# Up projections and first Strassen products of a two-branch attention step: other block order, weight tiles of two blocks, first sums on VectorE

## The chip, the cores and the metric

The kernel runs on one core of one Trainium2 chip. The metric is device time in microseconds (us) of one execution. A core has TensorE (PE; PEld is its weight loads), VectorE (DVE), ScalarE (ACT), GpSimd (POOL) and SyncE (SP), whose queue issues nearly all DMAs. Each engine works through its own list of instructions in order, and waits on semaphores for the others.

## The reference, cut to what matters

One layer of a decoder with two linear-attention branches over 1024 prompt tokens and 64 sample tokens (1088 columns in the kernel, which keeps features on the 128 partitions and tokens along the free dimension). The part that the change touches:

```
y_a = (o_a * silu(z_a)) @ w_up_gla          # 512 -> 1024
y_b = (o_b * silu(z_b)) @ w_up_gdn          # 512 -> 1024
merged = sigmoid(gate_a) * y_a + sigmoid(gate_b) * y_b
h = h + merged @ w_out                      # 1024 -> 1024
h = h + sigmoid(h @ w_ple_gate) * (p @ w_ple)
```

What goes before it (projections, the two recurrences) and after it (the last two lines, and a final RMS norm) is in the program too, and is left as it is.

## The kernel before, in words

**Products in three parts.** All matmuls are made in a reduced-precision fp32 form. A matrix is split into a high part (rounded by ScalarE, `A.copy`) and a low part (the difference, by VectorE), and a product takes three matmuls per block of 128 rows: high by high, high by low, low by high. So every operand of TensorE costs one ScalarE and one VectorE instruction beforehand. The helper for activations is `parts` (lines 1335 to 1337: L1336 the high part on ACT, L1337 the low part on DVE); that for weights is `w_split` (L174 and L175), which also starts the load of a later raw weight tile (`w_load`, L167). There are two raw weight tiles (`wr`) and three of each split kind (`wh`, `wl`).

**Up projections** (`up_block`, 16 calls). The 1024 output features are eight blocks m of 128, the branch is br (0 is GLA, 1 is gated DeltaNet), the columns are three chunks: c = 0 and 1 of 416, c = 2 of 256. One call handles one (br, m): it takes one split weight tile of 4 blocks (128x512), and for each chunk loads the gate that was spilled to DRAM earlier (`gt`, a buffer called strip, of which there are eight), makes 12 matmuls into a PSUM bank (`py`), and lets DVE apply the gate: for br = 0 one instruction writes the merged tile M (or Me for chunk 2; L1403); for br = 1 one multiplies (L1405) and one adds onto M (L1406). The list `UPS` sets the order of calls. Before, it is: blocks 0 and 4 of branch 0, then of branch 1; blocks 1 and 5 likewise; then blocks 2, 6, 3, 7 of branch 0, then the same four of branch 1.

**Strassen operands** (`m_parts`, L1408). The output projection `merged @ w_out` of the first 832 columns is done as a Strassen-Winograd product: 2x2 quadrants of M and of the weights, seven products instead of eight. The quadrants of M for row block j are b11, b12 (m = j, chunks 0 and 1) and b21, b22 (m = j + 4). `m_parts(j)` makes four sums T1 to T4 of them on GpSimd (`T`, L1414 to L1421) and splits seven operands (names `M11`, `MT2`, `MT3`, `MT1`, `M21`, `MT4`, `M22` with j behind), and splits the two blocks of chunk 2 (`M2h`, `M2l`). It can run only when blocks j and j + 4 of both branches are done, for j = 3 after the last up projection.

**Strassen products** (the loop over j that follows, line 1463 on). For each of four output row pairs j, TensorE makes the seven products in the order 1, 6, 7, 5, 2, 4, 3 (`s`, L1456, 12 matmuls each over the row blocks k = 0 to 3) with plain products for chunk 2 between them (`se`, `sf`, L1461). The weight quadrants are summed in `s_weights(j)`, on GpSimd (`sw`, L1358 to L1363), in four steps that `s_next` asks for. DVE and GpSimd combine the products with the residual x (strips again, loaded at L1469; adds on GpSimd at L1483, the rest on DVE at L1480).

**Order.** From the end of the first block of projections on, a scheduler at build time orders each engine's list by the order of the source and by dependencies. Buffers with the same tag are handed on when their last reader is done, and the next writer waits for that reader.

Of the kernel before, what the change touches and what calls it, by code (L numbers as in the profile page):

```python
# [17 lines left out]
P = 128  # L18
# [3 lines left out]
CH = [(0, 384), (384, 384), (768, 320)]  # L22
ORDER2 = (5, 6, 7, 0, 1, 2, 3, 4)
LCH = [(0, 416), (416, 416), (832, 256)]
UPS = [(i // 2 % 2, i // 4 + 4 * (i % 2)) for i in range(8)] + [(i // 4, 2 + i // 2 % 2 + 4 * (i % 2)) for i in range(8)]
EPS = 1e-6
NBLK = 34
NWARM = 3
# [76 lines left out]
def tile_hybrid_step(ctx: ExitStack, tc: tile.TileContext, xT, x0, pT, wqk, wmain, wv0, wv1, wup, wout, wpg, wpl, wgate,  # L105
# [16 lines left out]
    def unit(name, dt=F32):  # L122
        return up.tile([P, UW], dt, tag="u", name=name)
# [1186 lines left out]
    lp = ctx.enter_context(tc.tile_pool(name="lp", bufs=1))  # L1310

    assert len(gscr) == 16
    wlist += [(wup[8 * br + m], 4, P, hw_main) for br, m in UPS]
    wlist += [(wout[m], 8, P, None) for j in range(4) for m in (j, j + 4)]
    w_load()
    w_load()
# [18 lines left out]
    def parts(h, l, src):  # L1335
        A.copy(h, src)  # L1336
        V.tensor_tensor(l, src, h.bitcast(F32), op=ALU.subtract)  # L1337
# [5 lines left out]
    def s_weights(j):  # L1343

        r1, r2 = wraw.pop(0)[0], wraw.pop(0)[0]
        a11, a12, a21, a22 = r1[:, 0:4], r1[:, 4:8], r2[:, 0:4], r2[:, 4:8]
        s1, s2 = (lp.tile([P, 512], F32, tag="sw", name=f"sw{j}{i}", bufs=3).rearrange("p (k n) -> p k n", n=P) for i in range(2))

        def two(x, y):
            hl = hw_main(8, P)  # L1350
            out = []
            for i, z in enumerate((x, y)):
                h, l = (t[:, 4 * i:4 * i + 4] for t in hl)
                parts(h, l, z)
                out.append((h, l))
            return out

        G.tensor_tensor(s1, a21, a22, op=ALU.add)  # L1358
        G.tensor_tensor(s2, s1, a11, op=ALU.subtract)
        yield two(a11, s2)  # L1360
        G.tensor_tensor(a11, a11, a21, op=ALU.subtract)
        yield two(a11, s1)
        G.tensor_tensor(s2, a12, s2, op=ALU.subtract)  # L1363
        yield two(a12, a22)
        q = two(s2, a21)
        if j < 3:
# [17 lines left out]
    M2 = [lp.tile([P, 8, 256], F32R, tag="xb", name=f"M2{n}", bufs=2) for n in "hl"]  # L1384

    def mcols(m, c):
        o, w = LCH[c]
        return M[m][:, o:o + w] if c < 2 else Me[m // 4][:, w * (m % 4):w * (m % 4) + w]

    def up_block(br, m, og, prefetch):  # L1390
        us = w_next()
        if br == 0:
            M[m] = unit(f"M{m}") if m % 4 > 1 else lp.tile([P, 2 * W1], F32, tag="bs", name=f"M{m}", bufs=16)
        for c, (o, w) in enumerate(LCH):
            t = strip(f"gt{br}{m}{c}", w)
            load(t, gscr[f"{'gh'[br]}{m}"][:, o:o + w])
            if c == 0:
                prefetch()
            py = pps(f"py{br}{m}{c}")
            prod(py, w, us, 0, lambda k: og[0][k][:, o:o + w], lambda k: og[1][k][:, o:o + w], 4)  # L1400
            d = mcols(m, c)
            if br == 0:
                V.scalar_tensor_tensor(d, t, 1.0, py[:, :w], op0=ALU.add, op1=ALU.mult)  # L1403
            else:
                V.scalar_tensor_tensor(t, t, 1.0, py[:, :w], op0=ALU.add, op1=ALU.mult)  # L1405
                V.tensor_tensor(d, d, t, op=ALU.add)  # L1406

    def m_parts(j):  # L1408

        b11, b12, b21, b22 = mcols(j, 0), mcols(j, 1), mcols(j + 4, 0), mcols(j + 4, 1)  # L1410
        r = {p: Mp[p].__setitem__(j, pair(f"M{p}{j}", j > 1)) or Mp[p][j] for p in Mp}
        parts(*r["11"], b11)
        t1, t2, t3, t4 = (wide(f"T{i}{j}")[:, :W1] for i in range(4))
        G.tensor_tensor(t1, b12, b11, op=ALU.subtract)  # L1414
        G.tensor_tensor(t2, b22, t1, op=ALU.subtract)
        parts(*r["T2"], t2)
        G.tensor_tensor(t3, b22, b12, op=ALU.subtract)
        parts(*r["T3"], t3)
        parts(*r["T1"], t1)
        parts(*r["21"], b21)  # L1420
        G.tensor_tensor(t4, b21, t2, op=ALU.subtract)  # L1421
        parts(*r["T4"], t4)
        parts(*r["22"], b22)
        for m in (j, j + 4):
            parts(M2[0][:, m], M2[1][:, m], mcols(m, 2))

    og = [split_pairs(oa, "oga"), split_pairs(ob, "ogb")]
    for br in range(2):
        for c in range(3):
            og[br][2](c)  # L1430
    for i, (br, m) in enumerate(UPS):
        if i == 0:
            w_split()
        up_block(br, m, og[br], w_split if i < 15 else s_next)
        if br == 1 and m > 3:
            m_parts(m - 4)
    s_next()
    s_next()


    H, He = [None] * 8, [None] * 2
# [5 lines left out]
        return H[m][:, o:o + w] if c < 2 else He[m // 4][:, w * (m % 4):w * (m % 4) + w]  # L1447

    def h_parts(m, c):
        Hp[c][m] = pair(f"H{m}{c}", c == 1 and m < 2)  # L1450
        parts(*Hp[c][m], hcols(m, c))

    def s_prod(ps, a, b):
# [9 lines left out]
    for j in range(4):  # L1463
        last = j == 3
        x11, x12, x21, x22 = (strip(f"x{m}{c}") for m in (j, j + 4) for c in (0, 1))
        xe = [strip(f"x{m}2", 256) for m in (j, j + 4)]
        for t, m, c in ((x11, j, 0), (xe[0], j, 2), (x22, j + 4, 1), (x21, j + 4, 0), (xe[1], j + 4, 2), (x12, j, 1)):
            o, w = LCH[c]
            load(t, xT[m][:, o:o + w])  # L1469
        for m in (j, j + 4):  # L1470
            H[m] = lp.tile([P, 2 * W1], F32, tag="bs", name=f"H{m}", bufs=16) if j == 0 else unit(f"H{m}")
            if j == 0:
                He[m // 4] = lp.tile([P, UW], F32, tag="M", name=f"He{m // 4}", bufs=2)
        p1, u2, u3 = (wide(f"{n}{j}")[:, :W1] for n in ("p1", "u2", "u3"))

        def ps_(n):
            return pps(f"s{n}{j}")[:, :256 if n in "ef" else W1]

        def half_of(out, ps, x):
            V.scalar_tensor_tensor(out, ps, 0.5, x, op0=ALU.mult, op1=ALU.add)  # L1480

        def add(t, x):
            G.tensor_tensor(t, t, x, op=ALU.add)  # L1483

        (a11, s2) = queue.pop(0)
        ps = ps_("1")
        s_prod(ps, a11, "11")
        A.mul(p1, ps, 0.5)
        add(x11, p1)
        e = ps_("e")  # L1490
        c_prod(e, a11, 0, True)
        ps = ps_("6")
        s_prod(ps, s2, "T2")
        half_of(u2, ps, p1)
        s_next()
        (s3, s1) = queue.pop(0)
        ps = ps_("7")
        s_prod(ps, s3, "T3")
        half_of(u3, ps, u2)
        for t, u in ((x22, u3), (x12, u2), (x21, u3)):  # L1500
            add(t, u)
        ps = ps_("5")
        s_prod(ps, s1, "T1")
        half_of(hcols(j + 4, 1), ps, x22)
        half_of(x12, ps, x12)
        if last:
            pr = [unit(f"pr{k}") for k in range(2)]
            for k in range(2):
                load(pr[k][:, :T], pT[k])
            wlist += [(wpg[0], 8, P, hw_main)]  # L1510
# [12 lines left out]
        half_of(hcols(j, 0), ps, x11)
        if last:
            h_parts(3, 0)
        c_prod(e, a12, 4, False)
        half_of(hcols(j, 2), e, xe[0])
        ps = ps_("4")
        s_prod(ps, a22, "T4")
        half_of(hcols(j + 4, 0), ps, x21)  # L1530
        e = ps_("f")
        c_prod(e, a22, 4, True)
        if last:
            h_parts(7, 0)
# [12 lines left out]
        if not last:
            s_next()
# [124 lines left out]
def _layout(i):  # L1673
# [16 lines left out]
    def vcols(m):  # L1690
# [55 lines left out]
```

## Time and profile before

| what | value |
|---|---|
| three timed runs | median 1003.38 us (1003.37 to 1005.02) |
| the profiled execution | 1005.65 us, of which the span from the first to the last instruction is 1003.8 |
| granted TensorE clock, mean | 0.995 |
| busy: PE | 986.2 us, 98% of the span |
| busy: PEld | 953.7 us, 95% |
| busy: DVE | 655.4 us, 65% |
| busy: ACT | 414.4 us, 41% |
| busy: POOL | 94.4 us, 9% |
| DMA | 84.74 MB, mean 84 GB/s |

PE is busy nearly throughout, so the shares of the other engines say little by themselves: what matters is where PE stands still, or runs slowly, and who let it wait. A row of a timeline reads: start in us, duration, engine, line, operation, output <- inputs, and in brackets the idle time before it with the engine that ended it. A row of groups reads: count | busy us, mean ns of one | idle before. A row of stretches reads: from:to in us, length, then busy us (and instructions) of PE, PEld, DVE, ACT and POOL, the granted TensorE clock, the share of DMA, GB/s.

### The profile page before, as it was taken

The page shows a single profiled execution, that of the slowest core. Times are in us where ns is not written, and L with a number is a line of the kernel's source. Part 1 is how long each engine was busy: PE and PEld are TensorE (multiplying, and loading weights), DVE is VectorE, ACT ScalarE, POOL GpSimd, SP SyncE. Part 2 cuts the span into 40 slices and gives each one's busy share as a digit, 9 for nine tenths or more (in the row PEclk, how much of TensorE's full clock was granted, in tenths as well). Part 3 has the DMA queues.
Part 4 walks back from the last instruction along what each step waited for, and adds up shares of the span by engine and source line. Part 5 has one row for each costly group of instructions (what it writes and reads, how often), then busy time and mean ns, then how long its engine had stood idle before and what let it go on. Part 6 is the DMA issues. An engine that isn't in the chain of part 4 may idle for free.

```text
span 1003.8 us, 17776 instructions
## 1 busy us (share of the span) xinstructions
PE 986.2 (98%) x6968; PEld 953.7 (95%) x6968; DVE 655.4 (65%) x1441; ACT 414.4 (41%) x997; POOL 94.4 (9%) x107
## 2 busy tenths in 40 slices
PE   9999999999999999999999999999999799999996
PEld 8999999999999989899999999999999799999996
DVE  6885745332748959867876775567767855854356
ACT  7764634432524424452264323243223222643354
POOL 0000011010000000010001000000213553100000
PEclk9999999999999999999999999999999899999999
DMA  9011112231222130322132222014453333421024
GB/s 322 5 43 64 51 53 72 84 97 70 80 78 65 35 97 22 116 74 60 60 97 73 63 86 81 12 45 144 139 151 107 102 95 95 150 84 43 22 89 153
DMA packets 66395, 84.74 MB, mean 84 GB/s; under 512 B 27316, under 2 KB 51320, under 8 KB 66312
## 3 DMA queue, kind: packets, MB, share of 16 engines
q1 hardware_dynamic: 66024, 83.22, 26.7%
q8 instruction: 55, 0.90, 0.4%
q10 hardware_dynamic: 288, 0.39, 0.1%
q14 instruction: 28, 0.23, 0.1%
HBM read 65.38 MB, written 18.21 MB: 83 GB/s over the span
## 4 chain that ended last, share of the span: by engine, by line
PE 93%; DVE 4%; issue 1%; POOL 1%; ACT 0%; DVEq 0%; POOLq 0%
PE ing L290 12%; PE ingsh L290 10%; PE eg L290 10%; PE ingsg L290 9%; PE py L290 7%; PE s L1456 6%; PE inzb L290 5%; PE inza L290 5%; PE ep L290 2%; PE inka L290 2%; PE inqa L290 2%; PE v L406 2%; PE v L407 2%; PE v L409 2%; PE sf L1461 1%
## 5 line engine op out<-in xcount | busy, mean ns | idle before, releaser
L174 ACT CAST wh<-wr 128x1024 fp32r<-128x1024 f32 (+1 forms) x67 | 63.2, 947 | 130.5 <-PE py L290 42.8
L175 DVE TENSOR_TENSOR wl<-wr,wh 128x1024 fp32r<-128x1024 f32 (+1 forms) x67 | 74.9, 1119 | 63.8 <-ACT wh L174 63.0
L290 PE MATMUL ing<-xh,wh 128*128 128x384 f32 (+1 forms) x288 | 97.1, 337 | 0.0
L290 PE MATMUL ing<-xh,wl 128*128 128x384 f32 (+1 forms) x288 | 94.8, 329 | 0.0
L290 PE MATMUL ing<-xl,wh 128*128 128x384 f32 (+1 forms) x288 | 94.6, 329 | 0.0
L290 PE MATMUL eg<-H,wh 128*128 128x416 f32 x256 | 69.3, 351 | 0.0
L290 PE MATMUL ingsg<-xh,wh 128*128 128x384 f32 (+1 forms) x192 | 66.4, 346 | 0.0
L290 PE MATMUL ingsh<-xh,wh 128*128 128x384 f32 (+1 forms) x192 | 66.2, 345 | 0.0
L290 PE MATMUL ingsg<-xl,wh 128*128 128x384 f32 (+1 forms) x192 | 63.2, 329 | 0.0
L290 PE MATMUL ingsh<-xl,wh 128*128 128x384 f32 (+1 forms) x192 | 62.9, 328 | 0.0
L290 PE MATMUL ingsg<-xh,wl 128*128 128x384 f32 (+1 forms) x192 | 62.9, 327 | 0.0
L290 PE MATMUL ingsh<-xh,wl 128*128 128x384 f32 (+1 forms) x192 | 62.8, 327 | 0.0
L290 PEld LDWEIGHTS ing<-xh,wh 128*128 128x128 f32 x288 | 54.2, 188 | 0.9 <-issue 0.7
L290 PEld LDWEIGHTS ing<-xl,wh 128*128 128x128 f32 x288 | 54.2, 188 | 0.5 <-issue 0.5
L290 PEld LDWEIGHTS ing<-xh,wl 128*128 128x128 f32 x288 | 54.1, 188 | 0.2 <-issue 0.2
L798 DVE SCALAR_TENSOR_TENSOR D<-R,cw,D 128x1112 f32<-128x1112 f32 x36 | 49.3, 1369 | 2.4 <-ACT D L796 2.1
L290 PEld LDWEIGHTS eg<-H,wh 128*128 128x128 f32 x256 | 47.7, 188 | 0.3
L290 PE MATMUL eg<-H,wl 128*128 128x416 f32 x128 | 44.6, 348 | 0.0
L953 DVE TENSOR_TENSOR tm<-B 34x30 f32<-34x30 f32 (+14 forms) x120 | 38.3, 319 | 7.4 <-DMA B<-scra 5.3
L1456 PE MATMUL s<-MT,wh 128*128 128x416 f32 x128 | 36.8, 369 | 3.2 <-DVE MT L1337 2.1
L955 DVE TENSOR_TENSOR B<-B,tm 34x30 f32<-34x30 f32 (+14 forms) x120 | 38.2, 318 | 1.8
L290 PEld LDWEIGHTS ingsg<-xh,wh 128*128 128x128 f32 x192 | 36.2, 188 | 2.2 <-issue 1.7
(491 smaller groups left out, 2899.3 us busy)
## 6 DMA issues: line engine op xcount, KB each, us to landing
wr<-in_wmain SPq DMA_DIRECT2D x38, 512.0 KB, 3.5
wr<-in_wpg SPq DMA_DIRECT2D x13, 512.0 KB, 3.6
wr<-in_wup SPq DMA_DIRECT2D x16, 256.0 KB, 2.9
wr<-in_wout SPq DMA_DIRECT2D x8, 512.0 KB, 3.8
gt<-gscrg SPq DMA_DIRECT2D x16, 208.0 KB, 2.5
gt<-gscrh SPq DMA_DIRECT2D x16, 208.0 KB, 3.0
x<-in_xT SPq DMA_DIRECT2D x16, 208.0 KB, 2.4
out_yT<-y SPq DMA_DIRECT2D x8, 416.0 KB, 4.1
```

Of the source, the lines that this page charges most:

```text
L174: a = A.copy(wh, wr).ins
L175: b = (eng or V).tensor_tensor(wl, wr, wh.bitcast(F32), op=ALU.subtract).ins
L290: mm(ps[:, :w], l_, r_, start=i == 0, stop=i == len(seq) - 1)
L406: mm(ps[:, :n], h_, a_, start=k == 0, stop=False)
L407: mm(ps[:, :n], l_, a_, start=False, stop=False)
L409: mm(ps[:, :n], h_, b_, start=False, stop=k == 7)
L798: V.scalar_tensor_tensor(D[:, :n], R[:, i:n + i], cw[:, 4 * ci + i:4 * ci + i + 1], D[:, :n], op0=ALU.mult, op1=ALU.add)
L953: V.tensor_tensor(tv, Bv[:, j:j + 1, j + 1:32].broadcast_to([NBLK, j, n]), Bv[:, 0:j, j:j + 1].broadcast_to([NBLK, j, n]), op=ALU.mult)
L955: V.tensor_tensor(Bv[:, 0:j, j + 1:32], Bv[:, 0:j, j + 1:32], tv, op=ALU.add)
L1456: mm(ps, a[p_][:, k], Mp[b][k][q_], start=(k, i) == (0, 0), stop=(k, i) == (3, 2))
L1461: mm(ps, a[p_][:, k], M2[q_][:, k0 + k], start=first and (k, i) == (0, 0), stop=not first and (k, i) == (3, 2))
```

## The change

Five things are changed.

1. `UPS` now has eight entries (br, j) in the order (0,0), (1,0), (0,1), (1,1) and so on, and `up_pair` handles blocks j and j + 4 in one call, with one weight tile of 8 blocks (128x1024; the array is laid out anew on the host). Within a call the chunks come as (j,0), (j,1), (j+4,0), (j+4,1), (j,2), (j+4,2).
2. `m_parts` runs after each branch 1 call; its T sums go to VectorE; for j = 2 it splits 21 and 22 first, otherwise in the order in which the products need them, with the weight steps put between for j = 3.
3. The weight sums of `s_weights(0)` and the residual adds of j = 0 go to VectorE; j = 1 to 3 stay on GpSimd.
4. For j = 3 the merged tiles M take four of the eight strips. Other buffers move between pools.
5. Two weight steps that stood behind the up projections are asked for inside the last `m_parts`.

```
-UPS = [(i // 2 % 2, i // 4 + 4 * (i % 2)) for i in range(8)] + [(i // 4, 2 + i // 2 % 2 + 4 * (i % 2)) for i in range(8)]
+UPS = [(0, 0), (1, 0), (0, 1), (1, 1), (0, 2), (1, 2), (0, 3), (1, 3)]
-    wlist += [(wup[8 * br + m], 4, P, hw_main) for br, m in UPS]
+    wlist += [(wup[4 * br + j], 8, P, hw_main) for br, j in UPS]
...
+        E_ = V if j == 0 else G
-        G.tensor_tensor(s1, a21, a22, op=ALU.add)
-        G.tensor_tensor(s2, s1, a11, op=ALU.subtract)
+        E_.tensor_tensor(s1, a21, a22, op=ALU.add)
+        E_.tensor_tensor(s2, s1, a11, op=ALU.subtract)
...
-    def up_block(br, m, og, prefetch):
+    def up_pair(br, j, og, prefetch):
         us = w_next()
-        if br == 0:
-            M[m] = unit(f"M{m}") if m % 4 > 1 else lp.tile([P, 2 * W1], F32, tag="bs", name=f"M{m}", bufs=16)
-        for c, (o, w) in enumerate(LCH):
+        for m in (j, j + 4) if br == 0 else ():
+            if j == 3:
+                M[m] = [strip(f"M{m}{c}") for c in range(2)]
+            else:
+                t = unit(f"M{m}") if j == 2 else lp.tile([P, 2 * W1], F32, tag="bs", name=f"M{m}", bufs=16)
+                M[m] = [t[:, c * W1:c * W1 + W1] for c in range(2)]
+        for i, (m, c) in enumerate(((j, 0), (j, 1), (j + 4, 0), (j + 4, 1), (j, 2), (j + 4, 2))):
...
-            prod(py, w, us, 0, lambda k: og[0][k][:, o:o + w], lambda k: og[1][k][:, o:o + w], 4)
+            prod(py, w, us, m // 4 * 4, lambda k: og[0][k][:, o:o + w], lambda k: og[1][k][:, o:o + w], 4)
...
+        def put(p, src):
+            Mp[p][j] = pair(f"M{p}{j}", j == 3 or j == 2 and p not in ("21", "22"))
+            parts(*Mp[p][j], src)
+
+        if j == 2:
+            put("21", b21)
+            put("22", b22)
+        put("11", b11)
+        V.tensor_tensor(t1, b12, b11, op=ALU.subtract)
+        V.tensor_tensor(t2, b22, t1, op=ALU.subtract)
+        put("T2", t2)
         for m in (j, j + 4):
             parts(M2[0][:, m], M2[1][:, m], mcols(m, 2))
+        yield
+        V.tensor_tensor(t3, b22, b12, op=ALU.subtract)
+        put("T3", t3)
+        put("T1", t1)
+        yield
...
-    for i, (br, m) in enumerate(UPS):
-        if i == 0:
-            w_split()
-        up_block(br, m, og[br], w_split if i < 15 else s_next)
-        if br == 1 and m > 3:
-            m_parts(m - 4)
-    s_next()
-    s_next()
+    w_split()
+    for i, (br, j) in enumerate(UPS):
+        up_pair(br, j, og[br], w_split if i < 7 else s_next)
+        if br == 1:
+            for _ in m_parts(j):
+                if j == 3 and len(queue) < 3:
+                    s_next()
...
-            G.tensor_tensor(t, t, x, op=ALU.add)
+            (V if j == 0 else G).tensor_tensor(t, t, x, op=ALU.add)
```

TensorE's list holds the same number of instructions as before, and the Strassen products stand in the same order. The lists of the other engines move. Two places on VectorE are shown as the built programs have them, before and after apart.

The first is VectorE's list around the last up projections. In the names, `py172` is the product of branch 1, block 7, chunk 2, the last one; `gt172` is its gate; `M113` is the low part of operand 11 for j = 3, `MT23` that of T2; `Me1` and `M2l` belong to chunk 2; `wl` are low parts of weights. Before:

```order
L1405 SCALAR_TENSOR_TENSOR gt170_8446<-gt170_8446,py170_8458 128x416
L1337 TENSOR_TENSOR M113_8507<-M3_8132,M113_8507 128x416
L1406 TENSOR_TENSOR M7_8187<-M7_8187,gt170_8446 128x416
L1337 TENSOR_TENSOR M2l_7437<-Me0_7434,M2h_7436 128x256
L1337 TENSOR_TENSOR wl_8542<-wr_8305,wh_8541 128x512
L1405 SCALAR_TENSOR_TENSOR gt171_8473<-gt171_8473,py171_8475 128x416
L1337 TENSOR_TENSOR wl_8542<-sw00_8448,wh_8541 128x512
L1406 TENSOR_TENSOR M7_8187<-M7_8187,gt171_8473 128x416
L1405 SCALAR_TENSOR_TENSOR gt172_8490<-gt172_8490,py172_8492 128x256
L1337 TENSOR_TENSOR wl_8549<-wr_8305,wh_8548 128x512
L1406 TENSOR_TENSOR Me1_7435<-Me1_7435,gt172_8490 128x256
L1337 TENSOR_TENSOR MT23_8508<-T13_8517,MT23_8508 128x416
```

And after, from the gate of block 7, chunk 1 on (M113 stands five rows above the first row):

```order
L1411 SCALAR_TENSOR_TENSOR gt171_8410<-gt171_8410,py171_8412 128x416
L1412 TENSOR_TENSOR M71_8246<-M71_8246,gt171_8410 128x416
L1428 TENSOR_TENSOR T13_8462<-M71_8246,T03_8461 128x416
L1411 SCALAR_TENSOR_TENSOR gt132_8427<-gt132_8427,py132_8429 128x256
L1433 TENSOR_TENSOR T23_8463<-M71_8246,M31_8244 128x416
L1412 TENSOR_TENSOR Me0_7434<-Me0_7434,gt132_8427 128x256
L1411 SCALAR_TENSOR_TENSOR gt172_8444<-gt172_8444,py172_8446 128x256
L1337 TENSOR_TENSOR MT23_8470<-T13_8462,MT23_8470 128x416
L1412 TENSOR_TENSOR Me1_7435<-Me1_7435,gt172_8444 128x256
L1337 TENSOR_TENSOR M2l_7437<-Me0_7434,M2h_7436 128x256
L1337 TENSOR_TENSOR MT33_8485<-T23_8463,MT33_8485 128x416
```

Between the evacuations of the last blocks stood low parts of weights, and T13 was made on GpSimd; now the T sums stand there, the weights' low parts stand before the call and behind it, and both long chunks of block 7 come ahead of the two short ones.

The second place is further up, in the last steps of the DeltaNet recurrence, which TensorE makes between projections (`ch36` is its bank, `R23` the value that TensorE waits for next, `ztzb02` a gate of a projection). Before:

```order
L1261 SCALAR_TENSOR_TENSOR ztzb02_7178<-ztzb02_7178,inzb0_2_7131 128x320
L175 TENSOR_TENSOR wl_7503<-wr_7430,wh_7502 128x512
L1262 TENSOR_TENSOR ob0_4522<-ob0_4522,ztzb02_7178 128x320
L1036 SCALAR_TENSOR_TENSOR R23_6581<-ch36_7195,ned_163,R23_6581 128x128
L1042 TENSOR_SCALAR vn36_7208<-ch36_7195,brk3_5943 128x128
```

After:

```order
L175 TENSOR_TENSOR wl_7503<-wr_7430,wh_7502 128x1024
L1261 SCALAR_TENSOR_TENSOR ztzb02_7178<-ztzb02_7178,inzb0_2_7131 128x320
L1036 SCALAR_TENSOR_TENSOR R23_6581<-ch36_7195,ned_163,R23_6581 128x128
L1262 TENSOR_TENSOR ob0_4522<-ob0_4522,ztzb02_7178 128x320
L1042 TENSOR_SCALAR vn36_7208<-ch36_7195,brk3_5943 128x128
```

The first up weights' low part is twice as long and stands ahead of the recurrence's step; TensorE's matmul on R23 stands one matmul later.

More of the change, by code (lines that the diff above doesn't have):

```diff
@@ L1356, in two @@
             return out
-        G.tensor_tensor(s1, a21, a22, op=ALU.add)
-        G.tensor_tensor(s2, s1, a11, op=ALU.subtract)
+        E_.tensor_tensor(s1, a21, a22, op=ALU.add)
+        E_.tensor_tensor(s2, s1, a11, op=ALU.subtract)
         yield two(a11, s2)
-        G.tensor_tensor(a11, a11, a21, op=ALU.subtract)
+        E_.tensor_tensor(a11, a11, a21, op=ALU.subtract)
         yield two(a11, s1)
-        G.tensor_tensor(s2, a12, s2, op=ALU.subtract)
+        E_.tensor_tensor(s2, a12, s2, op=ALU.subtract)
         yield two(a12, a22)
@@ L1386, in mcols @@
     def mcols(m, c):
-        o, w = LCH[c]
-        return M[m][:, o:o + w] if c < 2 else Me[m // 4][:, w * (m % 4):w * (m % 4) + w]
-    def up_block(br, m, og, prefetch):
+        w = LCH[c][1]
+        return M[m][c] if c < 2 else Me[m // 4][:, w * (m % 4):w * (m % 4) + w]
+    def up_pair(br, j, og, prefetch):
         us = w_next()
-        if br == 0:
-            M[m] = unit(f"M{m}") if m % 4 > 1 else lp.tile([P, 2 * W1], F32, tag="bs", name=f"M{m}", bufs=16)
-        for c, (o, w) in enumerate(LCH):
+        for m in (j, j + 4) if br == 0 else ():
[5 more added lines that the diff above has]
+        for i, (m, c) in enumerate(((j, 0), (j, 1), (j + 4, 0), (j + 4, 1), (j, 2), (j + 4, 2))):
+            o, w = LCH[c]
             t = strip(f"gt{br}{m}{c}", w)
             load(t, gscr[f"{'gh'[br]}{m}"][:, o:o + w])
-            if c == 0:
+            if i == 0:
                 prefetch()
             py = pps(f"py{br}{m}{c}")
-            prod(py, w, us, 0, lambda k: og[0][k][:, o:o + w], lambda k: og[1][k][:, o:o + w], 4)
+            prod(py, w, us, m // 4 * 4, lambda k: og[0][k][:, o:o + w], lambda k: og[1][k][:, o:o + w], 4)
             d = mcols(m, c)
@@ L1410, in m_parts @@
         b11, b12, b21, b22 = mcols(j, 0), mcols(j, 1), mcols(j + 4, 0), mcols(j + 4, 1)
-        r = {p: Mp[p].__setitem__(j, pair(f"M{p}{j}", j > 1)) or Mp[p][j] for p in Mp}
-        parts(*r["11"], b11)
         t1, t2, t3, t4 = (wide(f"T{i}{j}")[:, :W1] for i in range(4))
[L1414 to L1423, printed above, removed]
+        def put(p, src):
[8 more added lines that the diff above has]
+        put("T2", t2)
         for m in (j, j + 4):
             parts(M2[0][:, m], M2[1][:, m], mcols(m, 2))
+        yield
[3 more added lines that the diff above has]
+        yield
+        if j != 2:
+            put("21", b21)
+        V.tensor_tensor(t4, b21, t2, op=ALU.subtract)
+        put("T4", t4)
+        if j != 2:
+            put("22", b22)
+        yield
     og = [split_pairs(oa, "oga"), split_pairs(ob, "ogb")]
@@ L1449, in h_parts @@
     def h_parts(m, c):
-        Hp[c][m] = pair(f"H{m}{c}", c == 1 and m < 2)
+        Hp[c][m] = pair(f"H{m}{c}", False)
         parts(*Hp[c][m], hcols(m, c))
@@ L1470, in tile_hybrid_step @@
         for m in (j, j + 4):
-            H[m] = lp.tile([P, 2 * W1], F32, tag="bs", name=f"H{m}", bufs=16) if j == 0 else unit(f"H{m}")
+            H[m] = unit(f"H{m}")
             if j == 0:
@@ L1702, in _layout @@
         xT=x.T.reshape(8, P, T), x0=x.T.reshape(8, P, T)[:, :, :384], pT=p.T.reshape(2, P, T), wqk=wqk, wmain=wmain, wv0=wv0, wv1=wv1,
-        wup=np.concatenate([blocks(a["w_up_gla"][0]), blocks(a["w_up_gdn"][0])], 0),
+        wup=np.concatenate([blocks(a["w_up_gla"][0]), blocks(a["w_up_gdn"][0])], 0)
+        .reshape(2, 2, 4, P, 4, P).transpose(0, 2, 3, 1, 4, 5).reshape(8, P, 8, P),
         wout=blocks(a["w_out"][0]), wpg=blocks(a["w_ple_gate"][0]), wpl=wpl, wgate=a["w_gla_gate"][0], pcols=pcols,
```

## The prediction

> **What bounds the kernel now.** I read the stretches first, then PE's waits, then PE's timeline, then the lists of the engines that PE waited for. The stretches of the last third (columns as told above; the two numbers before GB/s are the granted clock and the DMA share):
>
> ```profile
> 683.60:778.71 95.11, 95.11 (x579) 94.54 (x578) 67.84 (x115) 24.27 (x47) 19.16 (x15) 1.00 0.48 143
> 778.71:800.17 21.46, 15.98 (x75) 14.73 (x74) 20.26 (x31) 7.19 (x15) 11.28 (x9) 0.84 0.33 100
> 800.17:873.87 73.70, 73.70 (x458) 73.26 (x457) 45.41 (x72) 25.91 (x48) 29.89 (x24) 1.00 0.36 108
> 873.87:994.60 120.73, 120.73 (x727) 119.20 (x726) 63.85 (x112) 54.37 (x100) 0.00 (x0) 1.00 0.24 80
> 994.60:1003.80 9.20, 1.34 (x8) 0.80 (x6) 4.16 (x10) 3.36 (x9) 0.00 (x0) 0.83 0.38 114
> ```
>
> These are the up projections, the Strassen products up to product 2 of j = 0, the other Strassen products, the last products, and the tail. PE has no gap in the first, third and fourth and runs at full clock there; the tail isn't touched; only the second has gaps, and a clock of 0.84. So only there can this change win time, and in the others only lose it. PE's waits between 640 and 900 us (us in total, times, longest) are three, all on operands of j = 3 (`M` is M11, `MT` is T2):
>
> ```profile
> PE s L1456 <- DVE M L1337: 2.3, 1, 2.3
> PE s L1456 <- DVE MT L1337: 2.1, 1, 2.1
> PE s L1456 <- ACT MT L1336: 1.1, 1, 1.1
> ```
>
> What the stretch costs in all, PE's timeline tells by comparing j = 0 with j = 1, which does the same products:
>
> ```profile
> 778.71 0.54 PE L1456 MATMUL s<-M,wh 128*128 128x416 f32 x2
> ...
> 783.07 0.46 PE L1456 MATMUL s<-M,wh 128*128 128x416 f32 x1 [2.31 <-DVE M L1337]
> 787.90 0.46 PE L1456 MATMUL s<-MT,wh 128*128 128x416 f32 x1 [1.06 <-ACT MT L1336]
> 790.46 0.72 PE L1456 MATMUL s<-MT,wh 128*128 128x416 f32 x1 [2.10 <-DVE MT L1337]
> 800.16 0.28 PE L1461 MATMUL se<-M2h,wh 128*128 128x256 f32 x1
> 808.99 0.54 PE L1456 MATMUL s<-M,wh 128*128 128x416 f32 x2
> 821.73 0.28 PE L1461 MATMUL se<-M2h,wh 128*128 128x256 f32 x1
> ```
>
> From product 1 to the second part of `se`, j = 0 takes 800.16 - 778.71 = 21.45 us, j = 1 takes 821.73 - 808.99 = 12.74. The loss is 8.71 us: 2.31 + 1.06 + 2.10 = 5.47 of waiting, and 3.24 in which matmuls ran slowly. The five-us stretches show the slow clock right behind the waits:
>
> ```profile
> 785.00:790.00 5.00, 2.29 (x12) 1.67 (x10) 5.00 (x6) 1.76 (x4) 3.75 (x3) 0.90 0.41 116
> 790.00:795.00 5.00, 4.54 (x13) 4.36 (x14) 5.00 (x9) 2.82 (x7) 1.46 (x1) 0.50 0.23 88
> 795.00:800.00 5.00, 5.00 (x26) 4.92 (x26) 3.80 (x6) 0.62 (x1) 3.56 (x3) 0.92 0.29 92
> ```
>
> Why operands were late, the timelines of DVE, ACT and POOL tell:
>
> ```profile
> 778.82 0.54 ACT L1336 CAST M<-M 128x416 fp32r<-128x416 f32 x1 [2.55 <-DVE M L1406]
> 779.54 1.55 DVE L1337 TENSOR_TENSOR wl<-sw,wh 128x512 fp32r<-128x512 f32 x1
> 781.85 1.16 DVE L1337 TENSOR_TENSOR M<-M,M 128x416 fp32r<-128x416 f32 x1
> 786.20 1.07 POOL L1415 TENSOR_TENSOR T<-M,T 128x416 f32<-128x416 f32 x1 [3.64 <-DVE M L1406]
> 788.95 2.45 DVE L1337 TENSOR_TENSOR MT<-T,MT 128x416 fp32r<-128x416 f32 x3
> ```
>
> The high part of M11 was there at 779.4, but its low part stood behind other work in DVE's queue until 781.85. T2 waited for block 7, the last to be done, then for POOL, ACT and DVE in turn. The operand sets of j = 2 and 3 can be made only after the fourteenth and the sixteenth of the sixteen calls of before; DVE was full (20.26 of 21.46 us).
>
> **The change part by part.** Durations (for a tile: min/median/max in ns; for a group: total, mean ns):
>
> ```profile
> L1405 DVE SCALAR_TENSOR_TENSOR gt<-gt,py 128x416 f32<-128x416 f32 x16 | 9.2, 582 | 6.1 <-PE py L290 6.1
> L1406 DVE TENSOR_TENSOR M<-M,gt 128x416 f32<-128x416 f32 x16 | 9.3, 589 | 0.4
> L1403 DVE SCALAR_TENSOR_TENSOR Me<-gt,py 128x256 f32<-128x256 f32 x8 | 3.3, 418 | 5.0 <-PE py L290 5.0
> L1337 DVE TENSOR_TENSOR MT<-T,MT x16: 577/581/1685, 710.3 to 791.8; 128x416 fp32r<-128x416 f32 x16
> L1337 DVE TENSOR_TENSOR wl<-sw,wh x12: 673/684/1551, 779.5 to 858.8; 128x512 fp32r<-128x512 f32 x12
> 775.37 0.58 DVE L1337 TENSOR_TENSOR M<-M,M 128x416 fp32r<-128x416 f32 x1
> 775.87 0.58 DVE L1337 TENSOR_TENSOR MT<-T,MT 128x416 fp32r<-128x416 f32 x1
> 821.89 1.43 PE se L1461 x12
> 823.32 2.27 PE s L1456 x12
> ```
>
> So 0.59 us for a 416-column instruction, 0.42 for 256, 0.68 for 512; queued ones follow each other at 0.50 instead of 0.58. A product takes PE 2.27 us, one of chunk 2 1.43. PE's work is the same, 95.11 us for the up projections.
>
> *Order by pairs.* Sets j = 0, 1, 2 are made after calls 2, 4, 6 of eight, each call 11.89 us (95.11 / 8). So only set 3 is left at the end. DVE's load from the start of call 6 to the low part of `Me0`, which product part `se` needs first: by the order 36 instructions of 416 columns, 13 of 256, 8 of 512, T sums and weight sums among them: 36 x 0.59 + 13 x 0.42 + 8 x 0.68 = 32.1 us. PE gives three calls and 3.3 us, 39.0. It fits, with 6.9 left.
>
> *The T sums and sums of j = 0 on DVE.* No row of before has them there. The lower bound is 0.50, the queued step; the upper 1.69 or 1.55, the longest of rows of the same size. I take 0.59 and 0.68, the rows of two fp32 inputs without POOL beside them: the long ones stand where POOL works (786.20 to 790 above), and POOL's list is empty there now until the weights of j = 1. Nothing is gained below these on the path.
>
> *The last call.* Let E be the end of the last up matmul. Needs, counted from E: product 1 reads M11 of j = 3 from its tenth matmul on (E + 1.7); `se` reads `M2l` of block 3 at E + 2.27 + 1.07 = 3.3; product 6 reads T2 at E + 2.27 + 1.43 + 1.7 = 5.4; products 7 and 5 each 2.27 later. M11 now needs only the first chunk, done 9.6 us before E. The tail: block 7's second chunk ends two short products, 2.86 us, before E. From there ten rows stand up to `M2l`: gate, add, T13, gate, T23, add, gate, MT23, add, M2l: five of 0.59, five of 0.42, 5.0 us, plus about 0.2 to a product's end: E + 2.3. The need is E + 3.3, so 1.0 is left; with queued steps about 1.7. MT23 is done before, MT33 0.6 later. Behind it T4 and 22 have over 8 us. So all three waits go, and nothing is late next; the tightest is `M2l`.
>
> *Weight tiles of two blocks.* Half as many splits, each twice as long, one call ahead: covered by 11.89 us of PE. The first of them moves into the recurrence (second order piece):
>
> ```profile
> 654.98 0.62 ACT L174 CAST wh<-wr 128x512 fp32r<-128x512 f32 x1 [0.80 <-PE inzb L290]
> 657.43 0.35 DVE L1036 SCALAR_TENSOR_TENSOR R<-ch,ned,R 128x128 f32<-128x128 f32 x1
> 658.42 0.38 PE L1040 MATMUL ch<-R,AT 128*128 128x128 f32 x2
> L175 DVE TENSOR_TENSOR wl<-wr,wh 128x1024 fp32r<-128x1024 f32 x1 | 1.2, 1216 | 0.0
> L174 ACT CAST wh<-wr 128x1024 fp32r<-128x1024 f32 x1 | 1.0, 1049 | 2.4 <-PE s L1456 2.4
> ```
>
> Cast to 656.03, low part to 657.25, one gate step of 0.5, R at 658.1 instead of 657.8; PE takes it at 658.42 or one matmul later. Cost 0, at most 0.3 if that cover is gone.
>
> *Strips and queues.* With M of j = 3 in four strips, the gate loads of the last calls wait on SP's queue for evacuations, and the x loads of j = 0 behind them; DVE's new adds wait for those. Issue to landing of gates (us):
>
> ```profile
> DMA to landing us min/median/max: 2.3/2.7/3.9
> ```
>
> A strip's round is 0.3 of issue, 3.9 at worst, and 1.2 of evacuation: 5.4 us, against 4 products, 9.1. The first x load may start when M11 is cast and T1 summed, some 5 us before E, lands by E - 1, and is added after product 1, past E + 2.3. Cost 0.
>
> *The slow clock* goes with the waits. [...]
>
> *Sum.* In the profiled execution's own time 1005.65 - 8.71 = 996.94. That execution stands 2.27 above the median of the three runs; against the median, 1003.38 - 8.71 = 994.7.
>
> **The rivals.**
> - *A short wait stays* (10%). If three of the ten rows before `M2l` were stretched as the longest above (1.1 us each), 3.3 less the margin of 1.0 is a wait of 2.3: 997.0, with the slow clock behind it 1000.2. For it: 1.0 us is a thin cover. Against: POOL is idle there.
> - *The slow stretch is not the waits' doing* (5%): only 5.47 is won, 997.9. Against it: the clock is 1.00 in all stretches without waits. [...]
> - *DVE is the bound and the wait only moves* (5%). PE waits again from 6.9 us more than I counted over the last three calls; 12.4 more give back the 5.47 of waiting, and with the slow clock the old loss: about 1003.4. For it: DVE was full at this place. Against: 32.1 of 39.0.
> - *The strips bind, slower* (4%). If the landing took L, ten gate loads in fours make 2.5 rounds, each late by L + 1.5 - 9.1; at L = 12 that is 11 us lost, 1003.38 - 8.71 + 11 = 1005.7. It decides from L = 11.1 on; the longest landing was 3.9.
>
> **How the numbers follow.** Forecast 76%: all waits go, 994.7. The runs of before lie 1.65 apart, so a median may stand 0.8 or so to either side; down from 994.7 that gives 993.7, rounded for the uncertainty of the 8.71. Upward the range takes in the slow stretch (997.9) and the smaller end of a wait that stays: 998.6. The bound rivals (9%) and the worse part of the first are left out. Two tenths of a per cent, 2.0 us, is about what a measurement can tell here. Faster by more: forecast, first and second rival, 0.91; within: DVE's bound, 0.05; slower: the strips, 0.04.
>
> **What would show it.** Right: PE has no wait on `s` or `se` between the up projections and 870 us, the clock stays at 1.00 there, the stretch from product 1 to the second `se` of j = 0 takes 12.7 us, no DVE row near E lasts over 0.7. Wrong: a wait of PE on `M2l` or `MT`; gates whose evacuation waits for DMA in the last two calls; DVE rows of T that last over 1 us; a slow clock without a wait ahead of it.

## The result, and the profile after

The changed kernel takes 997.34 us (median of four runs, 997.15 to 997.55), the kernel before 1003.58 (four runs, 1003.37 to 1005.02). The ratio is 0.9935, 95% interval 0.9918 to 0.9952: faster by 6.24 us. A later measurement gave the same ratio (0.9935, 0.9923 to 0.9948). The forecast was 994.7, the range 993.7 to 998.6: the direction is right and the time lies in the range, but the gain was put 2.5 us too high.

In the trace there is nothing left of the stall. PE has no wait at all between 640 and 900 us (the list of waits is empty there). The stretches (up projections; products up to product 2 of j = 0; the other Strassen products; the last products; the tail), each from its own first matmul on:

```profile
683.40:778.73 95.33, 95.33 (x578) 94.59 (x577) 71.61 (x137) 22.91 (x42) 0.00 (x0) 1.00 0.45 132
778.73:791.48 12.75, 12.75 (x74) 12.65 (x73) 12.32 (x26) 6.14 (x13) 0.00 (x0) 1.00 0.58 170
791.48:865.03 73.55, 73.55 (x457) 73.10 (x457) 44.51 (x71) 26.29 (x49) 29.87 (x24) 1.00 0.35 107
865.03:985.62 120.59, 120.59 (x726) 119.10 (x725) 63.86 (x112) 53.98 (x98) 0.00 (x0) 1.00 0.25 80
985.62:995.40 9.78, 1.56 (x10) 1.01 (x8) 4.16 (x10) 3.37 (x9) 0.00 (x0) 0.72 0.36 108
```

The second stretch went from 21.46 to 12.75 us, by 8.71; the clock is 1.00 up to the tail. The up projections take 0.22 more, what lies ahead of them 0.20 less (683.60 to 683.40), and all that follows the second stretch 0.29 more (1003.80 - 800.17 = 203.63, now 995.40 - 791.48 = 203.92). Together -8.40, the difference of the two spans (1003.8 and 995.4). So against the profiled execution of before nearly all came that was forecast. Against the median it did not, and that is what the experiments are about.

DVE's list around the end of the up projections, which is E = 778.73 us in this trace:

```profile
776.08 0.59 DVE L1411 SCALAR_TENSOR_TENSOR gt<-gt,py 128x416 f32<-128x416 f32 x1 [1.06 <-PE py L290]
776.71 0.59 DVE L1412 TENSOR_TENSOR M<-M,gt 128x416 f32<-128x416 f32 x1
777.33 0.59 DVE L1428 TENSOR_TENSOR T<-M,T 128x416 f32<-128x416 f32 x1
...
779.34 0.59 DVE L1337 TENSOR_TENSOR MT<-T,MT 128x416 fp32r<-128x416 f32 x1
779.84 0.42 DVE L1412 TENSOR_TENSOR Me<-Me,gt 128x256 f32<-128x256 f32 x1
780.18 0.42 DVE L1337 TENSOR_TENSOR M2l<-Me,M2h 128x256 fp32r<-128x256 f32 x1
```

DVE waits for PE here (1.06 us ahead of the gate of block 7's second chunk), not the other way about. T2 is there at 779.93, 1.2 us after E, and `M2l` of block 3 at 780.60. PE takes that one at 782.19:

```profile
782.07 0.28 PE L1478 MATMUL se<-M2h,wh 128*128 128x256 f32 x1
782.19 0.28 PE L1478 MATMUL se<-M2l,wh 128*128 128x256 f32 x1
```

### The profile page after: what moved, and what is told of

It is laid out like the page before. It is cut to its first block, busy times and chain, and to the rows that moved or that the text cites. A ratio compares the mean times of both kernels' runs of the same rounds, so it can differ in the third digit from the quotient of the medians.

```text
span 995.4 us, 17705 instructions
## 1 busy us (share of the span) xinstructions
PE 982.9 (99%) x6968; PEld 951.4 (96%) x6968; DVE 650.9 (65%) x1457; ACT 413.2 (42%) x989; POOL 64.0 (6%) x83
## 4 chain that ended last, share of the span: by engine, by line
PE 56%; DVE 2%; ACT 0%; issue 0%; DVEq 0%
PE eg L290 10%; PE py L290 10%; PE s L1473 6%; PE inzb L290 5%; PE ing L290 5%; PE ingsg L290 5%; PE ingsh L290 4%; PE ep L290 2%; PE inza L290 1%; PE sf L1478 1%; PE se L1478 1%; PE ch L1040 1%; PE ch L1044 1%; PE ch L1045 1%; PE ch L1034 0%; PE ch L1035 0%
## 5 line engine op out<-in xcount | busy, mean ns | idle before, releaser
L175 DVE TENSOR_TENSOR wl<-wr,wh 128x1024 fp32r<-128x1024 f32 x59 | 71.9, 1221 | 65.1 <-ACT wh L174 64.7
L174 ACT CAST wh<-wr 128x1024 fp32r<-128x1024 f32 x59 | 61.7, 1049 | 107.1 <-PE ing L290 25.4
L290 PEld LDWEIGHTS ingsh<-xh,wh 128*128 128x128 f32 x192 | 36.2, 188 | 1.8 <-issue 1.1
```

The source lines that it names most:

```text
L174: a = A.copy(wh, wr).ins
L175: b = (eng or V).tensor_tensor(wl, wr, wh.bitcast(F32), op=ALU.subtract).ins
L290: mm(ps[:, :w], l_, r_, start=i == 0, stop=i == len(seq) - 1)
```

## The experiments

Twelve kernels. "Stretch" is the time from the first matmul of product 1 to the second part of `se`, j = 0, in that kernel's trace; without waits it is 12.75 us. The last column is the ratio to the kernel before on the same chip with its 95% interval.

| kernel | median us (lowest to highest, runs) | waits of PE in the trace, us | stretch | ratio |
|---|---|---|---|---|
| before again | 1004.25 (1003.03 to 1005.14, 11) | 2.38, 1.07, 2.11 | 19.07 | 1.0002 (0.9993 to 1.0012) |
| old order, sums on VectorE | 1000.34 (999.48 to 1001.39, 5) | 2.67 | 15.68 | 0.9962 (0.9950 to 0.9975) |
| order of calls alone | 1002.12 (1000.63 to 1003.23, 11) | 0.69, 2.10 | 17.63 | 0.9980 (0.9971 to 0.9988) |
| changed, sums back on GpSimd | 997.40 (997.04 to 997.72, 5) | none | 12.99 | 0.9931 (0.9918 to 0.9943) |
| changed, old chunk order | 997.73 (996.91 to 997.88, 5) | none | 12.74 | 0.9933 (0.9921 to 0.9945) |
| changed, both of these undone | 996.95 (996.20 to 997.95, 5) | none | 12.73 | 0.9928 (0.9916 to 0.9941) |
| changed again | 997.33 (997.03 to 998.45, 5) | none | 12.75 | 0.9935 (0.9923 to 0.9948) |
| T2 x7, x9, x14, PE free | 997.33, 997.58, 997.74 (5 each) | none | other order | 0.9932, 0.9935, 0.9937 |
| T2 x9, PE's list held | 1000.52 (1000.28 to 1001.43, 5) | 1.97, 0.17 | 15.43 | 0.9964 (0.9950 to 0.9978) |
| T2 x14, PE's list held | 1005.04 (1004.40 to 1005.84, 11) | 5.10 | 20.97 | 1.0009 (1.0000 to 1.0018) |

**The kernel before, once more.** Why 6.2 us and not 8.7? Nothing is edited here.

> The kernel before, unchanged. Theory A (the slow clock varies): the three waits of the profiled execution (2.31, 1.06, 2.10 us, in all 5.47) are in every execution, but the slow clock behind them, 3.24 us there, is not, and the median holds less of it. Then most timed runs have a span of 1001.3 to 1001.8 us and a mean clock of 0.996 or 0.997, not 0.995; the time goes down where the clock goes up; and in the new trace the waits stay at 5.2 to 5.7 us in all, while the stretch from product 1 to the second se of j = 0 takes 18.2 to 20.5 us in place of 21.45 unless the clock is 0.995 again. Rival B (the changed kernel loses the 2.5 us outside this stretch): the timed runs have the same 0.995 and the stretch takes 21.4 us again, and the spans are 1003 to 1004. Rival C (the time outside the span): the spans are 1003 to 1004 while the times are 1003.4, so that under 1 us lies outside the span, against 2.15 us in the changed kernel.

The median came out as before (1004.25 us beside 1003.91 for 21 more runs of the same kernel), and the new trace gives the answer. Its waits (in total, times, longest), and then its stretch:

```profile
PE s L1456 <- DVE M L1337: 2.4, 1, 2.4
PE s L1456 <- DVE MT L1337: 2.1, 1, 2.1
PE s L1456 <- ACT MT L1336: 1.1, 1, 1.1
```

```profile
778.46:797.53 19.07, 13.52 (x74) 12.49 (x73) 19.07 (x28) 7.20 (x15) 9.16 (x7) 1.00 0.29 86
```

The same three waits, within 0.1 us, and a clock of 1.00 throughout: the slow clock isn't in this execution. The stretch is 19.07 us, 6.32 above 12.75, where the first trace had 8.71. And the 6.32 is not all waiting: the waits are 5.56. PE's busy time is 13.52 in place of 12.75, and this 0.77 is what the three waits cost beside their length. PE's timeline shows how:

```profile
786.29 0.35 PE L1456 MATMUL s<-MT,wl 128*128 128x416 f32 x1
787.71 0.45 PE L1456 MATMUL s<-MT,wh 128*128 128x416 f32 x1 [1.07 <-ACT MT L1336]
790.27 0.46 PE L1456 MATMUL s<-MT,wh 128*128 128x416 f32 x1 [2.11 <-DVE MT L1337]
790.56 0.35 PE L1456 MATMUL s<-MT,wl 128*128 128x416 f32 x1
```

In a run of matmuls one starts 0.19 us after the other, though each is 0.35 long; before a wait the last one runs to its end (0.16 lost), and after it the next starts 0.29 later (0.10 lost). That is 0.26 us for each wait. So the 8.71 of the first trace were 5.47 of waits, 0.77 beside them, and 2.47 of slow clock, and between the two traces only the 2.47 differ. The span of 1001.2 us, against 1003.8, is 2.6 shorter, and 2.4 of that are this stretch. That the slow clock is in one execution and not in the other, behind the same waits, is shown.

How often it is there came out otherwise than theory A had it. It had most runs at 0.996 or 0.997 with a span of 1001.3 to 1001.8; six of these eleven have 0.995, and only two spans are below 1002. Over 56 runs of the kernel before, 30 had a mean clock of 0.995 and a median of 1004.6 us, 26 had 0.997 or 0.998 and a median of 1003.4. The two medians are 1.2 us apart, half of the 2.47. The mean clock can't say why: it also holds the tail, whose clock was 0.83 in the first trace and 0.72 in that of the changed kernel, and a run at 0.997 may hold a short piece of slow clock. How much of it an untraced run had stays open.

Rival B falls for the most part: the stretch did not take 21.4 us again. But 0.3 us was lost in the changed kernel's other stretches, as told above. Rival C falls but for another 0.3: 1.83 to 1.95 us lie outside the span in these runs, 2.12 to 2.19 in those of the changed kernel.

**One half of the change: sums on VectorE, order of before.**

```
-        G.tensor_tensor(t1, b12, b11, op=ALU.subtract)
+        V.tensor_tensor(t1, b12, b11, op=ALU.subtract)
...
-        G.tensor_tensor(s1, a21, a22, op=ALU.add)
+        (V if j == 0 else G).tensor_tensor(s1, a21, a22, op=ALU.add)
...
-            G.tensor_tensor(t, t, x, op=ALU.add)
+            (V if j == 0 else G).tensor_tensor(t, t, x, op=ALU.add)
```

> The kernel before with its T sums, and the weight sums and residual adds of j = 0, on VectorE; the old order of the up projections stays. Theory: DVE, which was full (20.26 of 21.46 us), gets four T sums of 0.6 and four weight sums of 0.7 us more, with the low weights of product 7 behind all seven operands of j = 3: PE waits at M11, M2l and T2 and then 3 to 5 us for wl; in all 9 to 11 us of waits against 5.47, 1004 to 1009 us. Rival (POOL's chain was what made T2 late): the T sums are sooner done, the waits fall to 3 us or less, 999 to 1001.

My theory was wrong by 4 us and more: 1000.34, and one wait in place of three. DVE was given the sums as well and was done sooner. Its wait, and its stretch:

```profile
PE s L1456 <- ACT wh L1336: 2.7, 1, 2.7
```

```profile
778.99:794.67 15.68, 13.01 (x74) 12.57 (x73) 15.68 (x32) 6.95 (x14) 0.00 (x0) 1.00 0.30 90
```

32 rows of DVE in 15.68 us, 0.49 a row, where the trace above has 28 in 19.07, 0.68 a row. DVE "full" was in good part DVE held up. The rows of before, DVE first, then POOL, show by what:

```profile
768.22 1.77 DVE L1337 TENSOR_TENSOR wl<-wr,wh 128x512 fp32r<-128x512 f32 x1
...
781.35 0.57 DVE L1405 SCALAR_TENSOR_TENSOR gt<-gt,py 128x416 f32<-128x416 f32 x1
781.85 1.16 DVE L1337 TENSOR_TENSOR M<-M,M 128x416 fp32r<-128x416 f32 x1
782.93 0.58 DVE L1406 TENSOR_TENSOR M<-M,gt 128x416 f32<-128x416 f32 x1
...
786.31 1.51 DVE L1337 TENSOR_TENSOR wl<-wr,wh 128x512 fp32r<-128x512 f32 x1
```

```profile
768.09 1.35 POOL L1359 TENSOR_TENSOR sw<-sw,wr 128x512 f32<-128x512 f32 x1
...
781.17 1.39 POOL L1363 TENSOR_TENSOR sw<-wr,sw 128x512 f32<-128x512 f32 x1 [0.63 <-DVE wl L1337]
786.20 1.07 POOL L1415 TENSOR_TENSOR T<-M,T 128x416 f32<-128x416 f32 x1 [3.64 <-DVE M L1406]
```

The low part of M11 starts at 781.85 and lasts 1.16 instead of 0.58: POOL's sum ends at 782.56, and the row ends 0.45 later, about one row's length. The multiply by the gate at 781.35, which reads one operand from PSUM, isn't held up (0.57 us beside the same sum). By what means the sum holds up the low part, no run shows.

The rival had the right time and waits, but its reason, that POOL's chain made T2 late, fits only in part. What moved most is the point at which DVE merges the second chunk of block 7 (E is the end of the up projections, 778.71 before and 778.99 here):

```profile
785.48 0.58 DVE L1406 TENSOR_TENSOR M<-M,gt 128x416 f32<-128x416 f32 x1
```

```profile
778.52 1.08 DVE L1406 TENSOR_TENSOR M<-M,gt 128x416 f32<-128x416 f32 x2
```

The first row is before, the second here: merged at E + 7.35 and at E + 0.61. From there to the low part of T2 it takes about as long as it did, 4.4 and 4.0 us. From 767 us to the merge, the held-up rows of before are together 5.0 us longer than such rows are without POOL, and DVE idled another 1.7 for operands that POOL had summed. The scheduler also ordered DVE's rows otherwise here, and that was not taken apart from the holding. What is left is the wait of 2.67 us for weights of product 7, whose sum (L1361) now stands in DVE's list behind the operands of j = 3.

**The other half: the order of calls alone.**

```
-UPS = [(i // 2 % 2, i // 4 + 4 * (i % 2)) for i in range(8)] + [(i // 4, 2 + i // 2 % 2 + 4 * (i % 2)) for i in range(8)]
+UPS = [(br, j + q) for j in range(4) for br in range(2) for q in (0, 4)]
```

> The kernel before with nothing changed but the list of calls: blocks 0 and 4, 1 and 5, 2 and 6, 3 and 7 one after the other, branch 0 and branch 1 each; single weight tiles, old chunk order, sums on GpSimd. Theory (the order does it alone): M11 of j = 3 is made over 10 us before E; block 7's second chunk is merged at about E, T1 on POOL ends at E + 1.2, T2 is there at E + 2.5, needed at E + 5.4. No wait, 997 to 998 us. Rival: with single weight tiles and sums on POOL the low weights in DVE's list or POOL's sums come late, 1 to 2 us of waits, 999 to 1002.

1002.12 us: the order alone does not do it. M11's wait is gone, both waits for T2 remain. Its waits, and its DVE's list around E, which is 778.05 here:

```profile
PE s L1456 <- DVE MT L1337: 2.1, 1, 2.1
PE s L1456 <- ACT MT L1336: 0.7, 1, 0.7
```

```profile
776.01 1.78 DVE L1337 TENSOR_TENSOR wl<-sw,wh 128x512 fp32r<-128x512 f32 x1
777.71 0.58 DVE L1337 TENSOR_TENSOR M<-M,M 128x416 fp32r<-128x416 f32 x1
...
781.87 0.58 DVE L1406 TENSOR_TENSOR M<-M,gt 128x416 f32<-128x416 f32 x1
```

The low part of M11 is there at 778.29, in time for its need at E + 1.7. But block 7 is merged only at 782.45, 4.4 us after E, since weight steps still stand beside the last calls: POOL sums weights between 775.88 and 779.46, and DVE's rows there last up to 1.78 us. It is the rival's case, a little beyond its upper end (it had 1 to 2 us of waits and 1002 us; here are 2.79 and 1002.12).

**Parts of the change undone.** Three kernels: the changed one with all sums back on GpSimd; with the old chunk order; with both.

```
-        E_ = V if j == 0 else G
+        E_ = G
...
-        V.tensor_tensor(t2, b22, t1, op=ALU.subtract)
+        G.tensor_tensor(t2, b22, t1, op=ALU.subtract)
...
-            (V if j == 0 else G).tensor_tensor(t, t, x, op=ALU.add)
+            G.tensor_tensor(t, t, x, op=ALU.add)
```

> The changed kernel with the T sums, the weight sums of j = 0 and the residual adds of j = 0 on GpSimd again; the order by pairs, the tiles of two blocks and the chunk order stay. Theory: the order does it alone. The last T1 can start on POOL 1.6 us before the end E of the up projections, ends at E - 0.5, with cast and low part T2 is there at E + 1.2 to 2.5, needed at E + 5.4; M2l is there by E + 2.6, needed at E + 3.3. No wait of PE, 996.9 to 998.0 us, within 0.1% of the changed kernel. Rival (the place of the sums matters): POOL and DVE slow each other, M2l or MT is late by 1 to 2 us, and the slow clock comes back: 998.5 to 1002.

```
-        for i, (m, c) in enumerate(((j, 0), (j, 1), (j + 4, 0), (j + 4, 1), (j, 2), (j + 4, 2))):
+        for i, (m, c) in enumerate(((j, 0), (j, 1), (j, 2), (j + 4, 0), (j + 4, 1), (j + 4, 2))):
```

> The changed kernel with the chunks of a call in the old order (j,0), (j,1), (j,2), (j+4,0), (j+4,1), (j+4,2); sums on VectorE. The second chunk of block 7 is merged at E in place of E - 1.6. Theory: T2 is there at E + 2.4, needed at E + 5.4; no wait, 997.0 to 997.8, the last chunks behind buy nothing here. Rival (the three short products at the end are needed to empty DVE's list): a wait at M2l or MT of 1 us or more, 998.3 to 1000.

> The same old chunk order with the sums on GpSimd again (so pairs and tiles of two blocks alone are left of the change). In the run with pairs and single tiles PE still waited 2.8 us for T2, since DVE, stretched to 1.0 to 1.8 us a row beside POOL, merged block 7 only 3.9 us after E. Theory A (that backlog came from the low weights of single tiles in DVE's list): no wait here, 997 to 998. Theory B (it came from the rows stretched beside POOL at the old chunk order): 1.5 to 3 us of waits for T2 again and 999 to 1002.5, spread over 1 us.

All three are as fast as the changed kernel, and none has a wait in the list. So neither the place of the sums nor the last chunks behind is needed once the rest is there: pairs, tiles of two blocks, and the weight steps ahead of the last call. In the third kernel POOL's weight sums for j = 0 were over before 765 us, and DVE was not behind when block 7 came (its second chunk):

```profile
776.53 0.59 DVE L1411 SCALAR_TENSOR_TENSOR gt<-gt,py 128x416 f32<-128x416 f32 x1 [0.81 <-PE py L290]
777.16 0.59 DVE L1412 TENSOR_TENSOR M<-M,gt 128x416 f32<-128x416 f32 x1
```

Merged at 777.75, which is this trace's E, in place of E + 4.4 with the order of calls alone. It went as theory A had it; but whether the tiles do it, or the earlier weight steps, the order within `m_parts` or the other pools, was not taken apart. With the sums on GpSimd and the new chunk order nothing is left of the time in hand, though: `M2l` of block 3 ended at 781.88, PE took it at 781.93, and the stretch is 0.24 longer.

**A wait put back.** To price the slow clock by itself, T2 of j = 3 is made 7, 9 and 14 times in the changed kernel, beside the changed kernel itself.

```
-        V.tensor_tensor(t2, b22, t1, op=ALU.subtract)
+        for _ in range(14 if j == 3 else 1):
+            V.tensor_tensor(t2, b22, t1, op=ALU.subtract)
```

> The changed kernel, unchanged, beside the three below on the same chip. Without waits there is nothing for the slow clock to follow: 997.0 to 997.8 us in every run, spread under 1 us, while the kernel before spreads over 2 us or more again.

> The changed kernel with the sum T2 of j = 3 made 7 times in place of once on DVE (the same result each time), so that MT23 is there 0.8 us too late for product 6 and nothing else is late. [...]

> The same with T2 made 9 times: one wait of 2.0 to 2.6 us at MT23, no other. [...]

> The same with T2 made 14 times: one wait of 4.5 to 5.1 us, as much as the three waits of the kernel before together, in one piece. [...]

The changed kernel spread over 1.4 us (I had said under 1) at a mean clock of 0.997 or 0.998 throughout, the kernel before over 2.7. The other three missed their aim: no wait arose. The scheduler knew of the longer chain and put other products into the gap. PE's list with T2 made 14 times, behind the third quarter of product 6:

```
L1474 MATMUL s60_8568<-MT22_8225,wl_8506 128x416
L1474 MATMUL s70_8592<-MT30_7737,wh_8491 128x416 x2
L1474 MATMUL s70_8592<-MT30_7737,wl_8492 128x416
...
L1474 MATMUL s50_8609<-MT10_7740,wh_8491 128x416 x2
```

PE could have gone on with T2 at 784.59 us and took it at 789.87, yet the 5.28 us between cost 0.4 at most (997.74 against 997.33), less than the 1.4 by which the changed kernel's runs spread. So I held PE's list in the order of the source for j = 0; it is then, matmul for matmul, that of the changed kernel.

```
+    pe_order = ExitStack()
+    pe_order.enter_context(tc.manual_schedule(engines={ET.PE}))
     for j in range(4):
+        if j == 1:
+            pe_order.close()
```

> The changed kernel with the sum T2 of j = 3 made 9 times in place of once (the same result each time), and PE's list held to the order of the changed kernel, so that no other product fills the gap: by DVE's rows MT23 is there at E + 7.7, needed at E + 5.4: one wait of 2.0 to 2.8 us, no other. [...]

> The same with T2 made 14 times: MT23 at E + 10.2, one wait of 4.5 to 5.3 us, as long as the three of the kernel before together (5.47), in one piece. [...] Against the kernel before (1003.7): if one gap is as dear as three, the median is within 1 us of it.

With 9 sums the waits are 1.97 and 0.17 us, the clock in the trace is 1.00, and the stretch is 15.43: 12.75 + 2.14 + 2 x 0.26 = 15.41. The runs spread over 1.15 us, the longest at a mean clock of 0.996, the others at 0.997 or 0.998; but in the traces of this study product 1 starts anywhere from 777.75 to 779.61 us, so a spread of this size doesn't tell whether the longest had the slow clock. With 14 sums there is one wait:

```profile
789.33 1.34 PE L1474 MATMUL s<-MT,wh 128*128 128x416 f32 x2 [5.10 <-ACT MT L1336]
```

All eleven runs have a mean clock of 0.993 to 0.996, and six of them are above 1005. The slow clock, from the wait of 5.10 us, then from the order of calls alone (behind waits of 0.69 and 2.10), then from the first profile of the kernel before:

```profile
788.42:795.24 6.82, 5.91 (x16) 5.34 (x17) 6.19 (x13) 4.18 (x9) 0.00 (x0) 0.50 0.19 50
```

```profile
787.60:791.00 3.40, 3.40 (x12) 3.27 (x11) 3.40 (x6) 1.63 (x4) 1.47 (x1) 0.50 0.04 12
```

```profile
788.98:795.80 6.82, 5.34 (x15) 5.13 (x16) 6.82 (x12) 3.84 (x9) 2.93 (x3) 0.50 0.24 91
```

In these three traces it comes in one piece of 3.40 or 6.82 us, at 0.50, and what it costs I estimate as half of the time in which PE works within it: 5.34 / 2 = 2.67 in the kernel before (2.47 by the stretch), 3.40 / 2 = 1.70 with the order of calls alone (17.63 - 12.75 - 2.79 - 0.52 = 1.57). One gap of 5.10 us was dearer than three of 5.47 together: 7.7 us above the changed kernel against 6.4 (1003.74 for before beside it); every one of its runs has a lower mean clock, of the kernel before only some. Shorter gaps did it too: with the order of calls alone the clock fell behind 0.69 and 2.10. The runs of the order of calls alone show the varying price too: from 1000.63 and 1001.20 us at a mean clock of 0.998 to 1003.23 at 0.993. Even with the single wait of 2.67 us (old order, sums on VectorE), two of five runs had 0.995 and took 0.95 to 1.91 us longer than the other three; neither was traced. What decides, behind short gaps, whether the slow clock comes was not shown.

## Why the prediction was right, and where it was off

- *What bounds the kernel: one stretch, three waits.* Right. All that was won was won there.
- *The loss is 8.71.* Right for that execution: the same stretch takes 12.75 us now. In that execution's own time the forecast was 996.94; the profiled execution of the changed kernel took 997.55. Of the 0.6 between, 0.3 lie in the other stretches (8.71 against 8.40) and 0.3 outside the span (997.55 - 995.4 = 2.15 against 1.85).
- *Sum: against the median, 1003.38 - 8.71 = 994.7.* This is the step that failed. It took the stall of one execution off the median of others, though the text itself had that this execution "stands 2.27 above the median". The term that was mis-sized is the 3.24 "in which matmuls ran slowly". 0.77 of it, draining and refilling PE, is in both traces; the other 2.47, the slow clock, is whole in the one and absent in the other. The 1003.38 is the time of a run without that much of it: the runs of before with the higher clock have a median of 1003.4, and one of 1003.03 was traced at 1.00. With 5.56 + 0.77 = 6.33 in place of 8.71: 1003.38 - 6.33 = 997.05. With the 0.6 us of the bullet above that the forecast left out, 997.7. Measured: 997.34, between the two; what is left is less than the runs of either kernel spread.
- *The range, 993.7 to 998.6.* That it holds 997.34 is luck in part. For the forecast's own mechanism it had 0.8 to either side of 994.7; the room above that was made for a slow stretch or a short wait that stays, and neither was there.
- *The slow clock goes with the waits.* Right: from 683 us up to the tail it is 1.00 in every stretch without a wait in the first trace and in that of the changed kernel, and from 700 to 800 us in the traces of the three kernels with parts undone, none of which waits. That it comes with them every time is what the text took for granted, and it doesn't. The rival by which it would stay (997.9) came nearer in its number than the forecast, by a mechanism that did not occur.
- *T sums on DVE at 0.59 and 0.68.* Right in size, all rows around E lie at 0.58 to 0.69 for these shapes. But none of it was needed, as the kernel with the sums back on GpSimd shows. By themselves the sums on VectorE won 3.6 us, the order of calls by itself 1.8; the two cure the same stall.
- *DVE's load, 32.1 of 39.0.* Right in size; the 39.0 us up to PE's need of `M2l`:

```profile
743.20:782.19 38.99, 38.99 (x238) 38.68 (x237) 31.80 (x63) 12.05 (x24) 0.00 (x0) 1.00 0.35 100
```

The 31.80 agree by two errors that cancel: there are 63 rows where 57 were counted, and rows in a queue follow at about 0.50 us.

- *The tail: `M2l` at E + 2.3, needed at E + 3.3.* 780.60 is E + 1.87 and 782.19 is E + 3.46: 1.6 us in hand where 1.0 was counted, as rows in a queue follow at 0.50.
- *The weight tile in the recurrence: 0 to 0.3.* 0: PE takes R at 658.38, before at 658.42. *The strips: 0.* Right: gates land 4.7 us after issue at worst, and DVE waited for one of them once, for 0.3 us.

## What to carry to other kernels

A stall read from one profile is that execution's stall. Split it into waits (each with 0.26 us for draining and refilling here) and slow clock. The waits came back within 0.1 us in a second profile here, the slow clock did not: a second profile of the kernel before tells the two apart, and a profiled execution that stands above the median is a reason to take one before the whole stall is counted as gain. And before an engine is called full, divide its busy time by its rows: rows of twice their usual length (1.16 us for 0.58, 1.51 to 1.77 for 0.68, each beside a GpSimd sum) say that it may be held up by a neighbour, and then moving work onto it can make it faster, as here.

## What the runs showed of the hardware

- The clock fell to 0.50 for 3.40 or 6.82 us, and did so with short gaps too: once behind gaps of 0.69 and 2.10 us, once behind gaps of 2.31 and 1.06 us and within the third, of 2.10. The same three gaps left it at 1.00 in another execution. With a gap of 5.10 us it fell in the trace, and all eleven runs have a mean clock of 0.993 to 0.996, where the changed kernel has 0.997 or 0.998.
- A wait of PE cost 0.26 us beside its length: 0.77 for three waits (1.07 to 2.38 us), and with one wait of 2.67 us the stretch is 15.68 = 12.75 + 2.67 + 0.26.
- VectorE rows with two SBUF inputs beside a GpSimd sum lasted 0.9 to 1.8 us instead of 0.58 to 0.69 (416 and 512 columns); a row with a PSUM input beside the same sum took its usual 0.57.
- Of the build and not of the chip: a scheduler that knew of a late operand hid 5.3 us of it for 0.4 at most. The waits of the kernel before were ones that it had not filled; that it reckoned with unstretched rows there is likely, and was not tested.
